# A two-layer hybrid decoder trunk in fp32 on one core: products of one width in runs, one PSUM bank less in each wino_job, and other numbers in the plan

## The chip, the cores and the metric

The kernel runs on one NeuronCore of a Trainium2 chip. The metric is the time of one execution on the device in microseconds; of several executions the median is taken. The engines are named as in the profile: PE (TensorE, matrix products; PEld are its weight loads), DVE (VectorE), ACT (ScalarE), POOL (GpSimd) and SP (SyncE, here only a queue that issues transfers).

## The reference, cut to what matters

Two layers, each of a mixer (retention and a Mamba-2 scan side by side, joined by gates) and a SwiGLU feed-forward, on 256 rows of 1024 columns, all in fp32.

```python
D_MODEL, SEQ, DEPTH = 1024, 256, 2

def hybrid_mixer(h, ...):
    u = h @ w_in
    q, k, v, g_ret, z, xbc, dt, gate_ret, gate_ssd = split(u)
    yr = retention(rotary(q), rotary(k) * RET_DK ** -0.5, v)
    o_ret = (silu(g_ret) * norm(yr)) @ ret_out
    xs, bm, cm = split(silu(causal_dwconv(xbc, conv_w, conv_b)))
    ys = ssd_scan(xs * dtp, dtp * a, bm, cm) + d_skip * xs
    o_ssd = (norm(ys * silu(z)) * ssd_norm_w) @ ssd_out
    return (sigmoid(gate_ret) * o_ret + sigmoid(gate_ssd) * o_ssd) @ w_o

def swiglu(h, w_gate_up, w_down):
    gate, up = split(h @ w_gate_up)
    return (silu(gate) * up) @ w_down

for l in range(DEPTH):
    h = h + hybrid_mixer(rmsnorm(h, norm_mix_w[l]), ...)
    h = h + swiglu(rmsnorm(h, norm_ffn_w[l]), w_gate_up[l], w_down[l])
return rmsnorm(h, final_norm_w)
```

## The kernel before

**Products.** Every fp32 operand is split into a high part (wh, xh) and a rest (wl, xl), and a product of two is the sum of three PE products: high by high, high by rest, rest by high. split_piece does this for each piece of a weight of 128x1024: ACT writes wh (L507), DVE writes wl as raw minus wh (L530). Pieces land in four buffers raw, and up to seven split pieces are held.

There are three ways in which a projection is made. In tm_jobs the activations are the stationary side and 512 or 352 columns of a weight move (mm3, L546 to L548). In **fm_job** the weight is stationary and the activations move; it is used for q, k, the convolution's channels and part of the feed-forward. High and rest of the activations lie beside each other in the tile xT, so one product of 512 columns (wh by high and rest, L1025, and L1028 for the last of a block) does two of the three, and one of 256 columns (wl by high, L1026) does the third into the first half of the same bank. A job has two blocks b of 16 products, each into one PSUM bank: for k = 0 to 6 a wide and a narrow one, and for k = 7 the narrow one first. The job's follower (gathered) lets ACT copy the second half of the bank and DVE add the first.

The third way is **seven**: a product of 2x2 blocks by seven products instead of eight (Strassen's scheme in Winograd's form), named "11", "t1", "t2", "22", "t3", "21" and "t4", of twelve PE products each in plain order. Each of them adds into a PSUM bank, a, b, c1 or c2; bank a is used by four in turn, and is copied to a tile u1, u2 or u3 of the pool sx (four buffers) before the next may add to it. wino_job combines these with additions on DVE (upper, first, third). wino_job is used once in each layer's mixer (the gate gs) and twice in each feed-forward. out_wino uses the same seven, but puts c1 and c2 into banks of its own (into).

**What sets the order.** The kernel is planned when it is built: each stream of work is a generator that yields operations with an engine, an assumed duration and a priority, and Flow runs them through a small model of the engines. At each free engine it takes the ready operation of the lowest priority number, and writes its instruction. The order of every engine's queue is so fixed in the program; on the chip each engine follows its own queue, and waits where an input isn't there yet. The model has one number for the time when the transfers will be free (transfer). Two kinds of transfers were not in it: the wb loads on POOL (load_wb, a fixed 4000 ns; eight of them) and the seg loads of ssd_chunk on SP (1500 on the queue and a fixed 5000 ns; sixteen of them). Each brings one row to all 128 partitions. Changes of these numbers move instructions, but add none.

PSUM has eight banks: six named acc, two named tr.

Of the kernel before, what the change touches and what calls it, by code (L numbers as in the profile page):

```python
# [16 lines left out]
P = 128  # L17
D = 1024
# [174 lines left out]
def trunk_kernel(  # L193
# [68 lines left out]
    sxS, new_sx = pooled(tp, (P, 512), F32, "sx", 4)  # L262
    segS, new_seg = pooled(tp, (P, HPG, P), F32, "seg", 2)
# [231 lines left out]
    def split_piece(raw, m, turn, pr, src=None):  # L495
# [26 lines left out]
        if src is not None:  # L522
            wl = yield Op("act", 0.833 * m + 92, negative, pr)
            yield Op("pool", 1050, lambda: add(wl), pr)
            yield fl.transfer(512 * m, 4 * m, 2.2) - ADDS
            return wh[:, :m], wl[:, :m]
# [9 lines left out]
    def splitter(turn, k, n, ev, job, src, sem):  # L536
        def land(raw, landed):
            yield landed
            wh, wl = yield from split_piece(raw, k * n, turn, job - 0.7, src)
            fl.release(sem)  # L540
            fl.set(ev, tuple(a.rearrange("p (k n) -> p k n", k=k) for a in (wh, wl)))
        return land
# [90 lines left out]
    def transposed(src, n, dst, i, t, pr, plain=None, slack=0.0):  # L633
# [11 lines left out]
        v = yield pe(110 * n, pr, emit)  # L645
# [31 lines left out]
    def seven_sums(ops, op, parts, tag, pr, plain=None):  # L677
# [6 lines left out]
        for n in range(2):  # L684
            for t in range(NT):
                yield (plain[n][t] if plain else op.ready[parts[n]][t])
        for n in range(2):
            for t in range(NT):
                if plain:
                    x[n, t] = yield plain[n][t]  # L690
                else:
                    xh, xl = (a[:, :, t * P : (t + 1) * P] for a in op.at(parts[n])[:2])
                    yield sxS
                    x[n, t] = new_sx("plain")
                    v = x[n, t].rearrange("p (j t) -> p j t", j=4)
                    yield tt(512, pr, v, xh.bitcast(F32), xl.bitcast(F32), ALU.add)
        x11, x12, x21, x22 = x[0, 0], x[1, 0], x[0, 1], x[1, 1]
# [203 lines left out]
    GOT = ("a", "b", "c1", "c2", "u1", "u2", "u3")  # L901

    def seven(j, pe_pr, ops, got, into={}):
# [6 lines left out]
        bank = {"11": "a", "t1": "b", "t2": "a", "22": "c1", "t3": "a", "21": "c2", "t4": "a"}  # L910
        after = {"11": "u1", "t2": "u2", "t3": "u3"}
        wait = {"t2": "u1", "t3": "u2", "t4": "u3"}
        box = {}

        def product(q):
# [7 lines left out]
            for k in range(4):  # L923
                wh, wl = yield evs[q][k // 2]

                def emit():
                    if first and k == 0:
                        box[name] = new_acc()
                    mm3(into[name]() if name in into else box[name], xh[:, k, :], xl[:, k, :], wh[:, k % 2, :], wl[:, k % 2, :],
                        first and k == 0, k == 3 and name not in into, skip_group_check=name == "a")  # L930
# [4 lines left out]
            if q in after:  # L935
                fl.spawn(copied(after[q]))
# [3 lines left out]
        def copied(name):  # L940
            yield sxS
            u = new_sx()
            yield act(512, j - 1, u, box["a"], AF.Copy, psum=True)
# [4 lines left out]
    def wino_job(ops, *posts):  # L948
# [4 lines left out]
        def upper():  # L953
# [53 lines left out]
    def fm_job(xT, post):  # L1007
# [4 lines left out]
        for b in range(2):  # L1012
            fsl = slice(b * P, (b + 1) * P)
            yield accS
            ps = None
            for k in range(8):
                for t in range(NT):
                    yield xT.ready[k // 4][t]
                wh, wl = yield evs[k // 4]

                def emit():
                    a = new_acc() if ps is None else ps
                    xh, _, x = xT.at(k // 4)
                    if k < 7:
                        nc.tensor.matmul(a, lhsT=wh[:, k % 4, fsl], rhs=x[:, k % 4, :, :], start=k == 0, stop=False)  # L1025
                    nc.tensor.matmul(a[:, :SEQ], lhsT=wl[:, k % 4, fsl], rhs=xh[:, k % 4, :], start=False, stop=False)  # L1026
                    if k == 7:
                        nc.tensor.matmul(a, lhsT=wh[:, k % 4, fsl], rhs=x[:, k % 4, :, :], start=False, stop=True)  # L1028
                    return a

                ps = yield pe(mm_cost(512) + mm_cost(256) + 5, pe_pr + 0.5, emit)
                if b == 1 and k % 4 == 3:
                    fl.release(hlS)
            if b == 0:
# [266 lines left out]
    def layer(l, mix, nxt, opening=None):  # L1301
# [75 lines left out]
        def steps():  # L1377
# [34 lines left out]
            ps = yield pe(240, pr, sums)  # L1412
# [13 lines left out]
            ps = yield pe(430, pr, sums_t)  # L1426
# [49 lines left out]
        def retention(hd, dst, q_ev, k_ev):  # L1476
# [15 lines left out]
            ps = yield pe(1290, pr, scores)  # L1492
# [149 lines left out]
        def xs_post(g, jj):  # L1642
            def post(ps, second, j):
# [18 lines left out]
                tps = yield pe(440, j, emit)  # L1662
# [15 lines left out]
        def ssd_scores(g):  # L1678
# [14 lines left out]
            ps = yield pe(650, pr, scores)  # L1693
# [23 lines left out]
        def ssd_chunk(g, t, lp, pr, dtt, acs, dec, dr, prm, cb, xs, x0_ev):  # L1717
# [8 lines left out]
            sg = yield Op("sp", 1500, bring, lp)  # L1726
            yield 5000.0
# [10 lines left out]
            yield tt(1024, lp, sg, sg, cb[:, 2 * t, :].unsqueeze(1).broadcast_to([P, HPG, P]), ALU.mult)  # L1738
            yield sxS
            xdt = new_sx("xdt")  # L1740
            yield tt(512, lp, h3(xdt), h3(xs[:, t, :]), hb(dtt, t * NH, g), ALU.mult)
            yield sxS
            tail = new_sx("tail")
            dsb = prm[:, 2, g * HPG : (g + 1) * HPG].unsqueeze(2).broadcast_to([P, HPG, HD])
            yield tt(512, lp, h3(tail), h3(xs[:, t, :]), dsb, ALU.mult)
            if t == 1:
# [8 lines left out]
                ips = yield pe(856, pr, inter)  # L1755
# [13 lines left out]
            yps = yield pe(1780, pr, intra)  # L1769
# [195 lines left out]
        def seven_job(kind, c, added):  # L1965
            if kind == "z":
                z_begins(c)
# [340 lines left out]
```

## Time and profile before

| | us |
|---|---|
| median of 3 runs | 1253.91 |
| lowest, highest | 1252.53, 1253.92 |
| the profiled execution's own time | 1254.38 |
| its span in the trace | 1252.6 |

The page of the profile begins with the span and each engine's busy time. A row of a group reads: line, engine, operation, output tile <- input tiles, shapes, xcount, then busy time in all, mean ns of one, and the engine's idle time just before them with what ended it. A PE product is pipelined: its shown duration (some 390 ns for 512 columns) is longer than its distance to the next one, so the distances between starts tell how densely products stand. A row of the timeline reads: start in us from the span's begin, duration, engine, line, operation, tiles, shapes, and how many it merges.

### The profile page before, as it was taken

Reading aid. Unit: us, or ns where it says so; the run is one execution under the profiler, and the core shown is the slowest. Engines: PE = TensorE matmul, PEld = TensorE weight load, DVE = VectorE, ACT = ScalarE, POOL = GpSimd, SP = SyncE. Lnnn points to the kernel's source line nnn. Section 1 sums busy time; section 2 is a strip of 40 time slices with the busy share of each in tenths; the row PEclk is TensorE's granted clock in tenths of the full one; section 3 lists DMA queues with packets and bytes.
Section 4 is the critical chain, followed back from the end, with each engine's and each line's share of the span. In section 5 each row is a group of like instructions: output and inputs, shape, how many; then the busy total and the mean of one; then the engine's idle time right before and its main releaser. Section 6 shows DMA issues by size and latency. Waiting matters only on the chain.

```text
span 1252.6 us, 17625 instructions
## 1 busy us (share of the span) xinstructions
PE 1241.2 (99%) x6293; PEld 1052.1 (84%) x6293; DVE 1108.7 (89%) x1519; ACT 880.7 (70%) x1304; POOL 72.0 (6%) x92
## 2 busy tenths in 40 slices
PE   9999999999999999999999999999999999999997
PEld 7889888888888778888888898888888888888886
DVE  6998889889999979999788888888899998899996
ACT  6966778786766566776586676878877674776753
POOL 0000000001012001001000000000010110010000
PEclk9999999999999999999999999999999999999999
DMA  8748565466777658877776475555676686677872
GB/s 314 252 133 287 163 207 154 164 236 134 254 235 218 230 176 237 293 209 219 258 254 230 117 253 170 185 172 163 216 182 238 240 233 216 211 216 252 294 201 86
DMA packets 76343, 266.27 MB, mean 213 GB/s; under 512 B 8768, under 2 KB 9536, under 8 KB 76256
## 3 DMA queue, kind: packets, MB, share of 16 engines
q1 hardware_dynamic: 68272, 237.12, 55.1%
q0 software_dynamic: 7552, 27.38, 11.8%
q8 instruction: 49, 0.80, 0.2%
q10 hardware_dynamic: 432, 0.66, 0.1%
q14 instruction: 38, 0.31, 0.1%
HBM read 262.96 MB, written 2.16 MB: 212 GB/s over the span
## 4 chain that ended last, share of the span: by engine, by line
PE 87%; DVE 4%; ACT 4%; issue 2%; DMA 2%; POOL 0%; POOLq 0%; DVEq 0%; ACTq 0%
PE acc L546 18%; PE acc L548 17%; PE acc L547 17%; PE acc L1025 15%; PE acc L1026 9%; PE tr L642 2%; PE acc L1028 2%; PE yps L1765 2%; DVE wl L530 2%; ACT wh L507 2%; PE acc L868 1%; DMA raw<-in_w_rw_dram 1%; ACT seg L1733 1%; DMA raws<-in_w_sw_dram 1%; PE acc L1487 1%
## 5 line engine op out<-in xcount | busy, mean ns | idle before, releaser
L530 DVE TENSOR_TENSOR wl<-raw,wh 128x1024 fp32r<-128x1024 f32 (+2 forms) x387 | 458.4, 1197 | 51.1 <-ACT wh L507 47.2
L507 ACT ACTIVATE wh<-raw 128x1024 fp32r<-128x1024 f32 (+2 forms) x387 | 396.8, 1037 | 137.9 <-PE acc L548 27.7
L1025 PE MATMUL acc<-xT,wh 128*128 128x512 f32 x840 | 304.9, 400 | 0.0
L1026 PE MATMUL acc<-xT,wl 128*128 128x256 f32 x960 | 251.2, 281 | 0.0
L546 PE MATMUL acc<-wh,xT 128*128 128x512 f32 (+1 forms) x568 | 220.4, 388 | 0.0
L547 PE MATMUL acc<-wl,xT 128*128 128x512 f32 (+1 forms) x568 | 216.2, 381 | 0.0
L548 PE MATMUL acc<-wh,xT 128*128 128x512 f32 (+1 forms) x568 | 216.2, 381 | 0.0
L1026 PEld LDWEIGHTS acc<-xT,wl 128*128 128x128 f32 x960 | 181.2, 189 | 10.4
L1025 PEld LDWEIGHTS acc<-xT,wh 128*128 128x128 f32 x840 | 158.0, 188 | 31.8
L547 PEld LDWEIGHTS acc<-wl,xT 128*128 128x128 f32 x568 | 106.8, 188 | 20.2 <-issue 1.0
L548 PEld LDWEIGHTS acc<-wh,xT 128*128 128x128 f32 x568 | 106.6, 188 | 19.6
L546 PEld LDWEIGHTS acc<-wh,xT 128*128 128x128 f32 x568 | 106.7, 188 | 19.3 <-issue 1.2
L507 ACT ACTIVATE wh<-raws 128x1024 fp32r<-128x1024 f32 x80 | 83.7, 1057 | 35.0 <-DVE raws L230 12.8
L530 DVE TENSOR_TENSOR wl<-raws,wh 128x1024 fp32r<-128x1024 f32 x80 | 96.4, 1220 | 9.2 <-ACT wh L507 9.0
L546 PE MATMUL acc<-wh,A 128*128 128x512 f32 x224 | 89.3, 399 | 0.3 <-DVE cc L230 0.2
L548 PE MATMUL acc<-wh,A 128*128 128x512 f32 x224 | 87.4, 390 | 0.0
L547 PE MATMUL acc<-wl,A 128*128 128x512 f32 x224 | 87.3, 390 | 0.0
L233 DVE SCALAR_TENSOR_TENSOR cc<-cc,cv 128x255 f32<-128x255 f32 (+1 forms) x144 | 67.2, 478 | 4.5 <-ACT cc L223 3.7
L223 ACT ACT_TABLE_LOAD x39 | 50.0, 1283 | 3.4 <-DVE cc L233 2.8
L546 PEld LDWEIGHTS acc<-wh,A 128*128 128x128 f32 x224 | 42.1, 188 | 9.9 <-ACT sil L223 1.0
L548 PEld LDWEIGHTS acc<-wh,A 128*128 128x128 f32 x224 | 42.0, 188 | 8.9
L547 PEld LDWEIGHTS acc<-wl,A 128*128 128x128 f32 x224 | 42.1, 188 | 8.5 <-issue 0.2
(201 smaller groups left out, 2057.2 us busy)
## 6 DMA issues: line engine op xcount, KB each, us to landing
raw<-in_w_tm_dram SPq DMA_DIRECT2D x100, 512.0 KB, 4.2
raw<-in_w_fm_dram SPq DMA_DIRECT2D x80, 512.0 KB, 4.3
raw<-in_w_gf_dram SPq DMA_DIRECT2D x40, 512.0 KB, 4.7
raw<-in_w_gate_up_dram SPq DMA_DIRECT2D x32, 512.0 KB, 6.3
raw<-in_w_down_dram SPq DMA_DIRECT2D x28, 512.0 KB, 4.6
raw<-in_w_gr_dram SPq DMA_DIRECT2D x24, 352.0 KB, 3.6
seg<-acs SPq DMA_DIRECT2D x16, 512.0 KB, 4.5
raw<-in_ret_out_dram SPq DMA_DIRECT2D x16, 512.0 KB, 3.8
```

The costliest lines, as they stand in the source:

```text
L223: return Op("act", cost, lambda: nc.scalar.activation(out=out, in_=in_, func=func, **kw), pr, TABLES.get(func))
L233: return Op("dve", 1.04 * n + 130, lambda: nc.vector.scalar_tensor_tensor(out=out, in0=in0, scalar=scalar, in1=in1, op0=op0, op1=op1), pr)
L507: nc.scalar.activation(out=wh[:, :m], in_=raw[:, :m], func=AF.Copy)
L530: nc.vector.tensor_tensor(out=wl[:, :m], in0=raw[:, :m], in1=wh[:, :m].bitcast(F32), op=ALU.subtract)
L546: nc.tensor.matmul(ps, lhsT=lh, rhs=rh, start=first, stop=False, **kw)
L547: nc.tensor.matmul(ps, lhsT=lh, rhs=rl, start=False, stop=False, **kw)
L548: nc.tensor.matmul(ps, lhsT=ll, rhs=rh, start=False, stop=last, **kw)
L642: nc.tensor.transpose(out=ps[:, j * P : (j + 1) * P], in_=src[:, j * P : (j + 1) * P], identity=ident)
L1025: nc.tensor.matmul(a, lhsT=wh[:, k % 4, fsl], rhs=x[:, k % 4, :, :], start=k == 0, stop=False)
L1026: nc.tensor.matmul(a[:, :SEQ], lhsT=wl[:, k % 4, fsl], rhs=xh[:, k % 4, :], start=False, stop=False)
L1028: nc.tensor.matmul(a, lhsT=wh[:, k % 4, fsl], rhs=x[:, k % 4, :, :], start=False, stop=True)
L1765: nc.tensor.matmul(ps[:, i * HD : (i + 1) * HD], lhsT=sg[:, i, :], rhs=xdt[:, i * HD : (i + 1) * HD], start=True, stop=True)
```

## The change

Four things are done together. Line numbers in the kernel after the change are 1 to 15 higher.

1. fm_job: the order in a block is now four wide products and four narrow ones of the first half of k, then four narrow and four wide ones of the second half. They are planned two at a time.
2. seven and wino_job: where it isn't into other banks, "22" adds into bank b, behind "t1". Before that, ACT copies "t1" to a further sx tile, ub, and "22" waits for it. The addition of c1 goes, and the job holds three banks, not four.
3. The plan's numbers: the wb loads on POOL and the seg loads now go through transfer (the seg load with 450 on the queue and 850 ahead), and groups of fp32 products cost a little more (transposes 113.5 instead of 110 each, and so on).
4. Two guards of the plan: sxG lets either seven_sums or the pair of chunks of one ssd_group take sx buffers; split_piece can release its source earlier (this is for pieces that the lists here don't name).

The core of the diff:

```diff
@@ load_wb
-        yield fl.transfer(4 * P * D) if eng == "sp" else 4000.0
+        yield fl.transfer(4 * P * D)
@@ seven
-        bank = {"11": "a", "t1": "b", "t2": "a", "22": "c1", "t3": "a", "21": "c2", "t4": "a"}
+        bank = {"11": "a", "t1": "b", "t2": "a", "22": "c1" if into else "b", "t3": "a", "21": "c2", "t4": "a"}
         after = {"11": "u1", "t2": "u2", "t3": "u3"}
         wait = {"t2": "u1", "t3": "u2", "t4": "u3"}
+        if not into:
+            after["t1"] = wait["22"] = "ub"
...
-            yield act(512, j - 1, u, box["a"], AF.Copy, psum=True)
+            yield act(512, j - 1, u, box[of], AF.Copy, psum=True)
@@ wino_job, upper
             yield tt(512, j, u2, b, u2, ALU.subtract)
-            c1 = yield got["c1"]
-            yield tt(512, j, u2, c1, u2, ALU.add)
             fl.release(accS)
             fl.spawn(posts[1](0, u2, j, sxS))
+            ub = yield got["ub"]
             u3 = yield got["u3"]
-            yield tt(512, j, u3, b, u3, ALU.subtract)
-            fl.release(accS)
+            yield tt(512, j, u3, ub, u3, ALU.subtract)
+            fl.release(sxS)
@@ fm_job
-            for k in range(8):
...
-                    if k < 7:
-                        nc.tensor.matmul(a, lhsT=wh[:, k % 4, fsl], rhs=x[:, k % 4, :, :], start=k == 0, stop=False)
-                    nc.tensor.matmul(a[:, :SEQ], lhsT=wl[:, k % 4, fsl], rhs=xh[:, k % 4, :], start=False, stop=False)
-                    if k == 7:
-                        nc.tensor.matmul(a, lhsT=wh[:, k % 4, fsl], rhs=x[:, k % 4, :, :], start=False, stop=True)
...
-                ps = yield pe(mm_cost(512) + mm_cost(256) + 5, pe_pr + 0.5, emit)
+            for half, wide in ((0, True), (0, False), (1, False), (1, True)):
...
+                    for k in (k0, k0 + 1):
+                        if wide:
+                            nc.tensor.matmul(box[0], lhsT=wh[:, k, fsl], rhs=x[:, k, :, :],
+                                             start=(half, k) == (0, 0), stop=(half, k) == (1, 3))
+                        else:
+                            nc.tensor.matmul(box[0][:, :SEQ], lhsT=wl[:, k, fsl], rhs=xh[:, k, :], start=False, stop=False)
+
+                for k0 in (0, 2):
+                    yield pe(2 * mm_cost(512 if wide else SEQ) + (5 if wide else 0), pe_pr + 0.5, lambda: emit(k0))
@@ ssd_chunk
-            sg = yield Op("sp", 1500, bring, lp)
-            yield 5000.0
+            sg = yield Op("sp", 450, bring, lp)
+            yield 850.0
+            yield fl.transfer(4 * P * D)
...
+            if t == 0:
+                yield sxG
             yield sxS
             xdt = new_sx("xdt")
...
             yield sxS
+            if t == 1:
+                fl.release(sxG)
```

What this does to the order of the queues is shown at three places. In all, the numbers of instructions of PE, POOL and SP stay; ACT has six copies more and six table loads fewer (40 to 34 in the program), DVE six additions fewer.

The first place is PE's queue at the start of the feed-forward's first fm_jobs in layer 0 (xT holds the activations; tr are transposes of the job before). Before the change:

```order
L1026 MATMUL acc<-xT,wl 128x256
L642 MATMUL tr<-cst,sil 128x128 x4
L1025 MATMUL acc<-xT,wh 128x512
L1026 MATMUL acc<-xT,wl 128x256
L1025 MATMUL acc<-xT,wh 128x512
L1026 MATMUL acc<-xT,wl 128x256 x2
L1028 MATMUL acc<-xT,wh 128x512
L1025 MATMUL acc<-xT,wh 128x512
```

And after it, at the same place:

```order
L1036 MATMUL acc<-xT,wh 128x512 x4
L1039 MATMUL acc<-xT,wl 128x256 x8
L646 MATMUL tr<-cst,sil 128x128 x4
L1036 MATMUL acc<-xT,wh 128x512 x8
L646 MATMUL tr<-cst,sil 128x128 x4
```

The alternation of wide and narrow has gone; the last four wide ones of a block and the first four of the next make a run of eight, and the transposes fall between runs.

The second place is ACT's queue at the first seven of the same feed-forward, where sx<-acc of 128x512 is the copy of a bank and wh<-... are splits of weights. Before the change:

```order
L223 ACTIVATE sx<-acc 128x512
L507 ACTIVATE wh<-cc 128x1024
L223 ACTIVATE C<-sil 128x512
L507 ACTIVATE wh<-cc 128x1024
L507 ACTIVATE wh<-raw 128x1024 x2
L223 ACTIVATE sx<-acc 128x512
L507 ACTIVATE wh<-raws 128x1024 x2
L507 ACTIVATE wh<-raw 128x1024 x2
L223 ACTIVATE sx<-acc 128x512
```

After it:

```order
L223 ACTIVATE sx<-acc 128x512
L508 ACTIVATE wh<-cc 128x1024
L223 ACTIVATE C<-sil 128x512
L508 ACTIVATE wh<-cc 128x1024
L223 ACTIVATE sx<-acc 128x512
L508 ACTIVATE wh<-raw 128x1024 x2
L223 ACTIVATE sx<-acc 128x512
L508 ACTIVATE wh<-raws 128x1024 x2
L508 ACTIVATE wh<-raw 128x1024 x2
L223 ACTIVATE sx<-acc 128x512
```

The copy of "t1" (the second sx<-acc) has come in between; the splits keep their order.

The third place is DVE's queue in layer 0's second half of the mixer, ahead of the last group's product ips, which PE makes from xdt (sr holds decay factors, C the group's xs, yps its first chunk's product). Before:

```order
L230 TENSOR_TENSOR C<-yps,tail 128x512
L233 SCALAR_TENSOR_TENSOR sil<-sil,rz,wb 128x512 x2
L530 TENSOR_TENSOR wl<-raw,wh 128x1024 x3
L230 TENSOR_TENSOR Y<-tr,Y 128x4x128
L530 TENSOR_TENSOR wl<-raw,wh 128x1024
L230 TENSOR_TENSOR Y<-tr,Y 128x4x128
L230 TENSOR_TENSOR xdt<-xdt,sr 128x512
```

After:

```order
L233 SCALAR_TENSOR_TENSOR sil<-sil,rz,wb 128x512 x2
L533 TENSOR_TENSOR wl<-raw,wh 128x1024 x3
L230 TENSOR_TENSOR Y<-tr,Y 128x4x128
L533 TENSOR_TENSOR wl<-raw,wh 128x1024
L230 TENSOR_TENSOR C<-yps,tail 128x512
L230 TENSOR_TENSOR xdt<-xdt,sr 128x512
```

The chunk's own addition, C<-yps, has moved from the front of the weights' splits to the place just ahead of xdt<-xdt,sr, and one transpose's follower (Y<-tr,Y) has moved behind it.

More of the change, by code (lines that the diff above doesn't have):

```diff
@@ L262, in trunk_kernel @@
     sxS, new_sx = pooled(tp, (P, 512), F32, "sx", 4)
+    sxG = Sem(1)
     segS, new_seg = pooled(tp, (P, HPG, P), F32, "seg", 2)
@@ L523, in split_piece @@
             wl = yield Op("act", 0.833 * m + 92, negative, pr)
+            if sem:
+                fl.release(sem)
             yield Op("pool", 1050, lambda: add(wl), pr)
@@ L538, in land @@
             yield landed
-            wh, wl = yield from split_piece(raw, k * n, turn, job - 0.7, src)
-            fl.release(sem)
+            wh, wl = yield from split_piece(raw, k * n, turn, job - 0.7, src, sem)
+            if src is None:
+                fl.release(sem)
             fl.set(ev, tuple(a.rearrange("p (k n) -> p k n", k=k) for a in (wh, wl)))
@@ L686, in seven_sums @@
                 yield (plain[n][t] if plain else op.ready[parts[n]][t])
+        if not plain:
+            yield sxG
         for n in range(2):
@@ L696, in seven_sums @@
                     yield tt(512, pr, v, xh.bitcast(F32), xl.bitcast(F32), ALU.add)
+        if not plain:
+            fl.release(sxG)
         x11, x12, x21, x22 = x[0, 0], x[1, 0], x[0, 1], x[1, 1]
@@ L929, in emit @@
                     mm3(into[name]() if name in into else box[name], xh[:, k, :], xl[:, k, :], wh[:, k % 2, :], wl[:, k % 2, :],
-                        first and k == 0, k == 3 and name not in into, skip_group_check=name == "a")
+                        first and k == 0, k == 3 and name not in into, skip_group_check=name in ("a", "b"))
                 yield pe(3 * mm_cost(512), pe_pr + 0.5, emit)
@@ L935, in product, with copied @@
             if q in after:
-                fl.spawn(copied(after[q]))
+                fl.spawn(copied(after[q], name))
             elif name not in into:
                 fl.set(got[name], box[name])
-        def copied(name):
+        def copied(name, of):
             yield sxS
             u = new_sx()
-            yield act(512, j - 1, u, box["a"], AF.Copy, psum=True)
+            yield act(512, j - 1, u, box[of], AF.Copy, psum=True)
             fl.set(got[name], u)
@@ L1014, in fm_job, with emit @@
             yield accS
-            ps = None
-            for k in range(8):
+            box = []
+            for half, wide in ((0, True), (0, False), (1, False), (1, True)):
                 for t in range(NT):
[L1018 to L1023, printed above, removed]
-                    if k < 7:
-                        nc.tensor.matmul(a, lhsT=wh[:, k % 4, fsl], rhs=x[:, k % 4, :, :], start=k == 0, stop=False)
-                    nc.tensor.matmul(a[:, :SEQ], lhsT=wl[:, k % 4, fsl], rhs=xh[:, k % 4, :], start=False, stop=False)
-                    if k == 7:
-                        nc.tensor.matmul(a, lhsT=wh[:, k % 4, fsl], rhs=x[:, k % 4, :, :], start=False, stop=True)
-                    return a
-                ps = yield pe(mm_cost(512) + mm_cost(256) + 5, pe_pr + 0.5, emit)
-                if b == 1 and k % 4 == 3:
+                    yield xT.ready[half][t]
+                wh, wl = yield evs[half]
+                def emit(k0):
+                    if not box:
+                        box.append(new_acc())
+                    xh, _, x = xT.at(half)
+                    for k in (k0, k0 + 1):
[6 more added lines that the diff above has]
+                    yield pe(2 * mm_cost(512 if wide else SEQ) + (5 if wide else 0), pe_pr + 0.5, lambda: emit(k0))
+                if b == 1 and (half, wide) in ((0, False), (1, True)):
                     fl.release(hlS)
+            ps = box[0]
             if b == 0:
@@ L1738, in ssd_chunk @@
             yield tt(1024, lp, sg, sg, cb[:, 2 * t, :].unsqueeze(1).broadcast_to([P, HPG, P]), ALU.mult)
+            if t == 0:
+                yield sxG
             yield sxS
@@ L1742, in ssd_chunk @@
             yield sxS
+            if t == 1:
+                fl.release(sxG)
             tail = new_sx("tail")
@@ L1753, in inter @@
                     return ps
-                ips = yield pe(856, pr, inter)
+                ips = yield pe(882, pr, inter)
                 yield tt(512, lp, h3(x0), h3(ips), hb(dec, 0, g), ALU.mult)
```

20 lines of the change are left out of this document (9 added, 11 removed).

## The prediction

> **What bounds the kernel now.** I read the page first, for the share of each engine and the chain that ended last.
>
> ```profile
> span 1252.6 us, 17625 instructions
> PE 1241.2 (99%) x6293; PEld 1052.1 (84%) x6293; DVE 1108.7 (89%) x1519; ACT 880.7 (70%) x1304; POOL 72.0 (6%) x92
> PEclk9999999999999999999999999999999999999999
> PE 87%; DVE 4%; ACT 4%; issue 2%; DMA 2%; POOL 0%; POOLq 0%; DVEq 0%; ACTq 0%
> ```
>
> TensorE (PE) is busy for 99% of the span at the full granted clock, and 87% of the last chain is its own work. To see how much it can still lose or win by waiting, I cut the span into head, middle and tail, and then listed what PE waited for.
>
> ```profile
> 0.00:6.03 6.03, 4.71 (x15) 1.00 0.60 193
> 6.03:1246.01 1239.98, 1236.50 (x6281) 1.00 0.68 213
> 1246.01:1252.60 6.59, 0.00 (x0) 0.72 0.21 80
> PE idle L2181 <- DVE mhalf L2158: 1.3, 1, 1.3
> PE tr L642 <- DVE sil L233: 1.1, 2, 0.8
> PE tr L642 <- ACT wh L507: 0.9, 1, 0.9
> PE ips L1752 <- DVE xdt L230: 0.5, 1, 0.5
> PE tr L642 <- DVE D L230: 0.4, 1, 0.4
> PE acc L546 <- DVE cc L230: 0.2, 1, 0.2
> ```
>
> The first three rows give stretch, its length, PE's busy time with its count, clock, DMA share and GB/s. Between the first product at 6.03 and the end of the last at 1246.01 PE is idle for 1239.98 - 1236.50 = 3.5 us. The other rows (who waited for whom; total, times, longest) name 3.1 us of it; the 1.3 us belong to the warm-up in the head. So the span is 6.0 head, 1236.5 products, 3.5 waits and 6.6 tail. DVE and ACT, with 11% and 30% of slack, cost nothing unless they make PE wait. **A change pays only by making the stream of products itself shorter, or by those 3.5 us.**
>
> Busy time says nothing of how densely products stand, so I went to the starts in the timeline. One job of fm_job has two blocks of 16 products, eight of 512 columns (wide, L1025 and L1028) and eight of 256 (narrow, L1026). L1028 stands once in each block.
>
> ```profile
> L1026 PE MATMUL acc<-xT,wl 128*128 128x256 f32 x960 | 251.2, 281 | 0.0
> L1028 PE MATMUL acc<-xT,wh 128*128 128x512 f32 x120 | 47.7, 397 | 0.0
> 480.09 0.40 PE L1028 MATMUL acc<-xT,wh 128*128 128x512 f32 x1
> ...
> 496.76 0.40 PE L1026 MATMUL acc<-xT,wl 128*128 128x256 f32 x2
> 497.00 0.40 PE L1028 MATMUL acc<-xT,wh 128*128 128x512 f32 x1
> 497.24 0.40 PE L546 MATMUL acc<-wh,xT 128*128 128x512 f32 x1
> 497.47 0.39 PE L547 MATMUL acc<-wl,xT 128*128 128x512 f32 x1
> 497.70 0.39 PE L548 MATMUL acc<-wh,xT 128*128 128x512 f32 x1
> 497.93 0.39 PE L546 MATMUL acc<-wh,xT 128*128 128x512 f32 x1
> ```
>
> There are 120 blocks (960 narrow products, 120 times L1028). From the L1028 at 480.09 to that at 497.00 lie exactly six blocks with nothing between them: 16.91 / 6 = **2.818 us a block**, or 0.352 us for a wide and a narrow one. The comparison comes from the end of the kernel, where the same widths stand in runs of one width.
>
> ```profile
> 1238.86 0.39 PE L546 MATMUL acc<-wh,C 128*128 128x512 f32 x1
> ...
> 1242.03 0.39 PE L548 MATMUL acc<-wh,Y 128*128 128x512 f32 x1
> 1242.26 0.28 PE L546 MATMUL acc<-wh,C 128*128 128x256 f32 x1
> 1242.37 0.28 PE L547 MATMUL acc<-wl,C 128*128 128x256 f32 x1
> ...
> 1245.73 0.28 PE L548 MATMUL acc<-wh,Y 128*128 128x256 f32 x1
> ```
>
> Fifteen wide products take 1242.26 - 1238.86 = 3.40 us, 0.2267 each; 29 narrow ones take 1245.73 - 1242.26 = 3.47 us, 0.1197 each. Sum 0.346, against 0.352 in alternation.
>
> **The products in runs.** The number of products is the same; their order in a block goes from fifteen changes of width to two. Eight wide and eight narrow ones at the pace of runs are 8 x 0.2267 + 8 x 0.1197 = 2.771 us. What is left are the two seams. Behind a narrow one, the wide starts at 497.00, 497.24, 497.47, 497.70 and 497.93 are 0.93 apart over four, where a run would have 0.907: this seam costs 0.02, and the third step is back at the pace of a run. At the other seam the first narrow step, 1242.26 to 1242.37, is 0.11, so 0.01 is won. New block: 2.771 + 0.02 - 0.01 = 2.781 us. That is 0.037 less than 2.818, times 120: **4.4 us off PE's own stream**, which nothing else can hide, since PE is the bound and its inputs are already waiting there (L1026's idle time is 0.0).
>
> Bounds of this term. Without any seam it is 0.047 x 120 = 5.6 us. If all four wide products behind a narrow run stay slow by the 0.01 of 497.00 to 497.24, 0.03 more a block are lost and 0.007 x 120 = 0.8 us remains. On the far side, if every wide one of these jobs took the 0.24 of that step wherever it stands, the block would be 8 x 0.24 + 0.958 = 2.878 us and the change would lose 7.2 us. Against that stands the first wide product of such a job behind a run of wide ones:
>
> ```profile
> 516.29 0.39 PE L1025 MATMUL acc<-xT,wh 128*128 128x512 f32 x1
> 516.51 0.28 PE L1026 MATMUL acc<-xT,wl 128*128 128x256 f32 x1
> 516.63 0.40 PE L1025 MATMUL acc<-xT,wh 128*128 128x512 f32 x1
> 516.86 0.28 PE L1026 MATMUL acc<-xT,wl 128*128 128x256 f32 x1
> ```
>
> It takes 0.22; the next one, behind a narrow one, 0.23. The slowness hangs on the neighbour, not on the job, so I take 4.4.
>
> The Trainium skill speaks against any gain here: TensorE: Matmul & The Clock Gate, section Back-to-back issue gap, gives the isolated gap of a warm product as columns / 2.4 + 2.5 ns, by the width alone, which makes 215.8 and 109.2 ns. By it the order would not matter and this term would be 0. The trace has 0.227 and 0.120 in runs, more than the page, and a step that depends on its neighbour.
>
> **The sevens.** Six jobs of wino_job (two on gs, four in the feed-forward) now copy "t1" out of PSUM with ACT, and "22" adds into that same bank; one DVE addition each goes.
>
> ```profile
> L223 ACT ACTIVATE sx<-acc 128x512 f32<-128x512 f32 x36 | 21.3, 593 | 11.2 <-PE acc L548 8.0 <-DVE C L230 2.2 <-DVE tail L230 0.8
> L230 DVE TENSOR_TENSOR sx<-acc,sx 128x512 f32<-128x512 f32 x36 | 24.5, 686 | 2.7 <-ACT sx L223 2.2 <-PE acc L548 0.4
> L223 ACT ACT_TABLE_LOAD x39 | 50.0, 1283 | 3.4 <-DVE cc L233 2.8
> ```
>
> ACT gains 6 x 0.593 = 3.6 us and, in the new order, loses six table loads of 1.283 (7.7 us); DVE loses 6 x 0.686 = 4.1 us. Neither is on PE's path: 0. The new wait is that of "22" for the copy. Between "t1" and "22" stands "t2", twelve wide products, 12 x 0.2267 = 2.7 us, while the copy takes 0.6 and may have one split of a weight (1.05) ahead of it. The same kind of wait exists already ("t2", "t3" and "t4" wait for a copy with one product between, 36 times), and no ACT sx stands among PE's waits above. So 0; without that cover it would be 0.6 plus what stands ahead in ACT's queue, some 1.6 us for each of six, 10 us at the far end. The freed bank brings nothing, for no wait above is for a bank but the 0.2 us of acc L546.
>
> **The account of transfers and fp32 groups.** These are only numbers in the plan; the instructions and bytes remain. They move transfers and small pieces of work.
>
> ```profile
> seg<-acs SPq DMA_DIRECT2D x16, 512.0 KB, 4.5
> wb<-in_ssd_norm_w_dram POOLq DMA_DIRECT2D x4, 512.0 KB, 6.9
> wb<-in_norm_ffn_w_dram POOLq DMA_DIRECT2D x2, 512.0 KB, 4.1
> ```
>
> The plan took 4.0 us for wb; it lands after 4.1 to 6.9. On SP a few seg loads change place with one or two weights, on POOL almost nothing. What can come of it is bounded by PE's waits. Of the 3.1 us the 0.9 (tr for ACT wh, in the opening) and the 1.1 (tr for DVE sil, at the two feed-forward norms) are a latency with the same rows around it in the new order: they stay. The other 1.1 us (ips, tr for D, acc L546) stand where rows move. They may go, or as many new ones may come: I count 0 and +-1.5 us. The guards sxG hold back work in the plan, not on the chip: 0.
>
> **The sum.** 1254.38 (this execution: 1252.6 span and 1.8 around it) - 4.4 = 1250.0. This execution stands 0.4 above the median of the runs shown, 1253.91; so the median after is 1249.6. A measurement of this kernel tells 0.2%, 2.5 us, from no change.
>
> **Rivals.** (1) *A product's step goes by its width and job alone*, and reordering gives nothing: 1253.9, same. For it speaks that 0.006 us a pair is less than the timeline's two digits and comes from means over 96 and 44 products; against it the rows at 516. Chance 0.13; the rule quoted above from the Trainium skill would be this case. (2) *The gain is given back in new waits*: the plan was balanced on a few tenths (the waits above are all under 1 us), and rows move at sixteen seg loads. Four waits like the 0.5 of ips give 1251.6, same. For it: in the new DVE order the scaled xdt still stands only a few rows ahead of its ips. Chance 0.09. (3) *Slower: the four sx buffers.* A seven now holds u1, ub, u2 and u3 at once, which is all four; before, it held three. If another stream still holds one, ACT's copy of u3 waits at the head of ACT's queue until u1 is used, which is after product "21"; the splits of weights queue behind it, and "t4" starts late by the addition 0.69, the activation 0.6, the copy 0.59 and three handovers of about 0.2: 2.4 us. It decides from three of the six sevens on: 1249.6 + 3 x 2.4 = 1256.8; all six, 1264.0. Against it:
>
> ```profile
> 499.95 0.69 DVE L230 TENSOR_TENSOR sil<-sx,sil 128x512 f32<-128x512 f32 x1
> 511.05 0.60 ACT L223 ACTIVATE sx<-acc 128x512 f32<-128x512 f32 x1 [0.29 <-PE acc L548]
> ```
>
> At the first seven of the feed-forward the last outside reader of an sx is done at 500.64, and u3 is copied at 511.05, ten microseconds later. Chance 0.05, and 0.03 more for the wide products at 0.24 (1261 us).
>
> **How the numbers follow.** The forecast keeps 0.70: 1249.6, own range 1246.8 (5.6 won, 1.5 of waits gone) to 1252.6 (2.6 won, halfway between 0.8 and 4.4, and 1.3 of new waits). The range has to reach to rival 1, most of it: 1247.0 to 1253.5. Faster by over 0.2% (below 1251.4): 0.70, which is the forecast less its upper edge, 0.04, and some cases of rival 2, 0.04. Same: 0.21. Slower (above 1256.4): 0.09, rival 3 with its companion and a stray 0.01.
>
> **What would show it.** Right: a block of these jobs in the new timeline at 2.78 us (first wide start to the next block's), narrow runs at 0.12, wide ones back at 0.227 from the third on; PE's busy time down by 4 to 5 us, its idle time between 3 and 5 us, DVE down 4 us with no effect. Wrong: a block at 2.82 (rival 1), new rows of 0.5 us and more among PE's waits (rival 2), or rows "PE acc <- ACT sx" of 2 us at the sevens (rival 3). A stall in the opening or at a norm that grows past 2 us would also break the sum.

## The result, and the profile after the change

| | before | after |
|---|---|---|
| median, us | 1253.8 (1252.53 to 1254.87, 8 runs) | 1257.28 (1255.76 to 1258.54, 8 runs) |
| ratio after to before, 95% interval | | 1.0028 [1.0017, 1.0039] |
| the profiled execution, its span | 1254.38, 1252.6 | 1257.84, 1255.6 |

The change makes the kernel 3.5 us slower, a little over what can be told from no change. The forecast was 1249.6 with a range up to 1253.5. Of all executions below, one of e3 (1366.42 us, at a granted clock of 0.85) and one of e4 (2525.56 us) fell far out of line with the others; the medians include them, the ratios and intervals do not.

The page after the change: span, each engine's busy time, and the shares of the chain that ended last.

```profile
span 1255.6 us, 17609 instructions
PE 1239.3 (99%) x6293; PEld 1051.0 (84%) x6293; DVE 1104.5 (88%) x1513; ACT 873.0 (70%) x1304; POOL 75.3 (6%) x92
PE 70%; DVE 14%; issue 6%; DMA 5%; ACT 4%; POOL 1%; POOLq 0%; ACTq 0%; DVEq 0%; SPq 0%
```

PE is busy for 1.9 us less than before and still for 99%, but the chain reads differently: PE's own work is 70% of it, not 87%, and DVE 14%, not 4%. That hints at waits, but a share of the chain doesn't count them. The same cut as before, middle and tail (the head is 6.03 again; stretch, length, PE's busy time with its count, clock, DMA share, GB/s):

```profile
6.03:1249.38 1243.35, 1234.56 (x6279) 1.00 0.67 213
1249.38:1255.60 6.22, 0.01 (x1) 0.67 0.22 84
```

In the middle PE is idle for 1243.35 - 1234.56 = 8.8 us, where it was 3.5. Set against before: products 1236.5 to 1234.6, **1.9 us won**; idle 3.5 to 8.8, **5.3 us lost**; tail 6.6 to 6.2, 0.4 won. That is +3.0, the difference of the spans. The rest of +3.5 lies around the span (2.2 us, where it was 1.8). What PE waited for, in the list after the change:

```profile
PE acc L552 <- DVE A L230: 3.2, 2, 1.8
PE idle L2196 <- DVE mhalf L2173: 1.3, 1, 1.3
PE ips L1769 <- DVE xdt L230: 1.3, 2, 1.0
PE tr L646 <- ACT wh L508: 1.3, 1, 1.3
PE tr L646 <- DVE sil L233: 0.9, 3, 0.3
PE tr L646 <- DVE D L230: 0.7, 2, 0.4
PE yps L1782 <- DVE Y L230: 0.5, 1, 0.5
PE acc L551 <- DVE wl L533: 0.4, 1, 0.4
PE acc L1499 <- DVE C L230: 0.3, 1, 0.3
PE acc L550 <- ACT sx L223: 0.2, 1, 0.2
```

Without the warm-up (1.3, L2196, in the head) these are 8.8 us against 3.1, and the first row, which did not exist before, is 3.2 of the 5.7 that came in. It stands once in each layer, at w_o, whose stationary side A is the transposed mixer output: in layer 0 at the first products (1.75 us), in layer 1 seven microseconds further into them (1.41 us, behind two splits in DVE's queue). Here is PE's queue in layer 0, in the timeline after the change (tr are the transposes of D, A the tile that their result goes to):

```profile
423.02 0.60 PE L646 MATMUL tr<-cst,D 128*128 128x128 f32 x4
...
425.28 0.63 PE L646 MATMUL tr<-cst,D 128*128 128x128 f32 x4 [0.28 <-DVE D L230]
425.66 0.47 PE L550 MATMUL acc<-wh,A 128*128 128x512 f32 x1
425.98 0.40 PE L551 MATMUL acc<-wl,A 128*128 128x512 f32 x1
428.13 0.50 PE L552 MATMUL acc<-wh,A 128*128 128x512 f32 x1 [1.75 <-DVE A L230]
```

And DVE's, from the same timeline, with the row in which ACT copies the transposes to A:

```profile
423.32 1.21 DVE L533 TENSOR_TENSOR wl<-raw,wh 128x1024 fp32r<-128x1024 f32 x1
424.19 0.58 ACT L223 ACTIVATE A<-tr 128x512 fp32r<-128x512 f32 x1
424.45 0.68 DVE L230 TENSOR_TENSOR D<-D 128x512 f32<-128x512 f32 x1
425.06 0.68 DVE L230 TENSOR_TENSOR D<-acc,D 128x512 f32<-128x512 f32 x1
425.66 1.21 DVE L533 TENSOR_TENSOR wl<-raw,wh 128x1024 fp32r<-128x1024 f32 x1
426.79 0.68 DVE L230 TENSOR_TENSOR D<-D 128x512 f32<-128x512 f32 x1
427.39 0.68 DVE L230 TENSOR_TENSOR A<-tr,A 128x512 fp32r<-128x512 f32 x1
```

The transposes of 423.02 are done at 423.6. DVE's follower A<-tr,A subtracts ACT's copy from them, so it could run when that copy ends, at 424.8. In DVE's queue it stands behind two splits and three operations on D, and it starts at 427.39. PE has one L550 and one L551 to do before it needs A's low part, and waits for 1.75 us. The same place in the timeline before the change, both engines:

```profile
422.31 0.63 PE L642 MATMUL tr<-cst,D 128*128 128x128 f32 x4 [0.43 <-DVE D L230]
...
425.54 0.69 DVE L230 TENSOR_TENSOR A<-tr,A 128x512 fp32r<-128x512 f32 x1
...
426.71 0.40 PE L548 MATMUL acc<-wh,A 128*128 128x512 f32 x1
```

Before, PE came to its L548 4.4 us after the start of the transposes (twelve other products stood between them and the first product with A, not six), and DVE to its follower 3.2 us after it, not 4.4. ACT's copy ended at 423.6 there (422.97 and 0.60), so DVE's queue set the follower's start in both. The follower was done at 426.2, half a microsecond ahead of its reader. DVE has 12% of slack over the span and none here.

The runs of one width, in the timeline after the change:

```profile
480.08 2.00 PE L1036 MATMUL acc<-xT,wh 128*128 128x512 f32 x8
481.92 1.11 PE L1039 MATMUL acc<-xT,wl 128*128 128x256 f32 x8
...
494.04 2.00 PE L1036 MATMUL acc<-xT,wh 128*128 128x512 f32 x8
```

Five blocks take 494.04 - 480.08 = 13.96 us, 2.792 each: 0.026 under the 2.818 of alternation, where 0.037 was forecast.

So the part that was to win, wins, though by less than forecast, and PE's new waits take more than that back. The experiments ask which part of the change brings the waits, and whether any part costs something by itself.

### The profile page after: what moved, and what is told of

The parts are those of the page before. It is cut to its first block, busy times and chain, and to the rows that moved or that the text cites. A ratio compares the mean times of both kernels' runs of the same rounds, so it can differ in the third digit from the quotient of the medians.

```text
span 1255.6 us, 17609 instructions
## 1 busy us (share of the span) xinstructions
PE 1239.3 (99%) x6293; PEld 1051.0 (84%) x6293; DVE 1104.5 (88%) x1513; ACT 873.0 (70%) x1304; POOL 75.3 (6%) x92
## 4 chain that ended last, share of the span: by engine, by line
PE 70%; DVE 14%; issue 6%; DMA 5%; ACT 4%; POOL 1%; POOLq 0%; ACTq 0%; DVEq 0%; SPq 0%
PE acc L1036 15%; PE acc L550 14%; PE acc L552 14%; PE acc L551 14%; PE acc L1039 8%; DVE wl L533 6%; ACT wh L508 2%; PE yps L1782 2%; PE tr L646 2%; DVE D L230 1%; DMA raw<-in_w_fm_dram 1%; ACT seg L1746 1%; DMA raw<-in_w_rw_dram 1%; DVE cc L233 1%; DMA raws<-in_w_sw_dram 1%
## 5 line engine op out<-in xcount | busy, mean ns | idle before, releaser
L1036 PE MATMUL acc<-xT,wh 128*128 128x512 f32 x960 | 249.4, 394 | 0.0
L550 PE MATMUL acc<-wh,xT 128*128 128x512 f32 (+1 forms) x568 | 221.1, 389 | 0.0
L551 PE MATMUL acc<-wl,xT 128*128 128x512 f32 (+1 forms) x568 | 216.0, 380 | 0.4 <-DVE wl L533 0.4
L1036 PEld LDWEIGHTS acc<-xT,wh 128*128 128x128 f32 x960 | 171.0, 189 | 28.8
L1039 PEld LDWEIGHTS acc<-xT,wl 128*128 128x128 f32 x960 | 131.0, 190 | 9.4 <-issue 0.5
L1039 PE MATMUL acc<-xT,wl 128*128 128x256 f32 x960 | 137.0, 284 | 0.0
L551 PEld LDWEIGHTS acc<-wl,xT 128*128 128x128 f32 x568 | 106.8, 188 | 20.7 <-issue 1.2
L550 PEld LDWEIGHTS acc<-wh,xT 128*128 128x128 f32 x568 | 106.7, 188 | 20.0 <-issue 1.2
L550 PE MATMUL acc<-wh,A 128*128 128x512 f32 x224 | 88.6, 396 | 0.0
L551 PE MATMUL acc<-wl,A 128*128 128x512 f32 x224 | 87.2, 389 | 0.0
L233 DVE SCALAR_TENSOR_TENSOR cc<-cc,cv 128x255 f32<-128x255 f32 (+2 forms) x144 | 67.5, 478 | 7.5 <-ACT cc L223 6.8
L550 PEld LDWEIGHTS acc<-wh,A 128*128 128x128 f32 x224 | 42.1, 188 | 8.5 <-ACT sil L223 0.4
L223 ACT ACTIVATE sil<-acc 128x512 f32<-128x512 f32 (+1 forms) x60 | 31.0, 526 | 26.0 <-PE acc L552 14.1
L551 PEld LDWEIGHTS acc<-wl,A 128*128 128x128 f32 x224 | 42.1, 188 | 8.3
```

The costliest lines, as they stand in the source:

```text
L223: return Op("act", cost, lambda: nc.scalar.activation(out=out, in_=in_, func=func, **kw), pr, TABLES.get(func))
L233: return Op("dve", 1.04 * n + 130, lambda: nc.vector.scalar_tensor_tensor(out=out, in0=in0, scalar=scalar, in1=in1, op0=op0, op1=op1), pr)
L550: nc.tensor.matmul(ps, lhsT=lh, rhs=rh, start=first, stop=False, **kw)
L551: nc.tensor.matmul(ps, lhsT=lh, rhs=rl, start=False, stop=False, **kw)
L1036: nc.tensor.matmul(box[0], lhsT=wh[:, k, fsl], rhs=x[:, k, :, :], start=(half, k) == (0, 0), stop=(half, k) == (1, 3))
L1039: nc.tensor.matmul(box[0][:, :SEQ], lhsT=wl[:, k, fsl], rhs=xh[:, k, :], start=False, stop=False)
```

## The experiments

All medians are compared with the kernel before on the same chip (1253.7 to 1253.8 us). "Idle" and "busy" are PE's in the middle cut, made in one trace of each as above; e2, with the products of before, is 0.9 us less busy than before, so differences of that size in one trace say nothing.

| run | median | ratio, 95% interval | idle | busy |
|---|---|---|---|---|
| before | 1253.8 | | 3.5 | 1236.5 |
| after | 1257.28 | 1.0028 [1.0017, 1.0039] | 8.8 | 1234.6 |
| e1 runs in the old plan | 1251.21 | 0.9978 [0.9969, 0.9987] | 3.4 | 1234.0 |
| e2 sevens alone | 1254.01 | 1.0002 [0.9993, 1.001] | 3.4 | 1235.6 |
| e3 account alone | 1263.95 | 1.0074 [1.0061, 1.0087] | 9.1 | 1240.4 |
| e4 runs in a new plan | 1264.2 | 1.0079 [1.0066, 1.0092] | 10.8 | 1239.5 |
| e5 after, one number | 1254.88 | 1.0008 [0.9999, 1.0017] | 5.5 | 1234.3 |
| e6 after, other numbers | 1252.23 | 0.9993 [0.9984, 1.0002] | 2.6 | 1233.9 |
| e7 fp32 groups alone | 1268.81 | 1.012 [1.0106, 1.0134] | 13.0 | 1241.7 |
| e8 transfers alone | 1257.6 | 1.0031 [1.002, 1.0041] | 5.0 | 1238.2 |
| e9 runs of two | 1251.62 | 0.9981 [0.9972, 0.999] | 2.6 | 1234.2 |
| e10 runs and sevens | 1251.1 | 0.9977 [0.9968, 0.9986] | 3.3 | 1233.5 |
| e11 all, planned otherwise | 1254.63 | 1.0008 [0.9999, 1.0017] | 5.3 | 1234.8 |

### e1: the runs, with the plan of before

The plan still yields eight steps of "one wide and one narrow product", so every queue stays as it was. Only what a step writes follows a table (1 is wide, the second number is k):

```diff
+    RUNS = [[(1, 0), (1, 1)], [(1, 2)], [(1, 3), (0, 0)], [(0, 1), (0, 2), (0, 3)],
+            [(0, 4), (0, 5), (0, 6)], [(0, 7), (1, 4)], [(1, 5)], [(1, 6), (1, 7)]]
-                    if k < 7:
-                        nc.tensor.matmul(a, lhsT=wh[:, k % 4, fsl], ...)
-                    nc.tensor.matmul(a[:, :SEQ], lhsT=wl[:, k % 4, fsl], ...)
+                    for wide, i in RUNS[k]:
+                        if wide: ...
```

> The kernel before with its plan untouched: every queue keeps its order, only inside a block of fm_job the products stand as four wide, eight narrow, four wide. Theory A (the denser stream is worth 120 x 0.027 = 3.2 us wherever it is used, and the loss came with the new plan): 1250.6 us, PE's waits 3 to 4 us without the warm-up. Rival B (a denser stream only brings PE sooner to the same inputs, so the gain comes back as waits): 1253 to 1254 us, waits 6 to 7 us.

1251.21 us, 2.6 less than before. The middle of its trace:

```profile
6.03:1243.37 1237.34, 1233.98 (x6279) 1.00 0.68 214
```

And the starts of two runs of wide products in its timeline, four blocks apart:

```profile
480.97 2.00 PE L1029 MATMUL acc<-xT,wh 128*128 128x512 f32 x8
...
492.14 2.00 PE L1029 MATMUL acc<-xT,wh 128*128 128x512 f32 x8
```

Four blocks in 11.17 us, 2.793 each, and PE's busy time is 2.5 us lower with the same idle time. The runs of one width alone are worth 2.6 us, by the products themselves. Rival 1, that a product's step goes by its own width and job alone, is out.

### e2: the sevens, with the plan of before

Only bank and copy in seven and wino_job, and the guard sxG, with which this was planned:

```diff
+        bank = {..., "22": "c1" if into else "b", ...}
+        if not into:
+            after["t1"] = wait["22"] = "ub"
```

> The kernel before with the sevens on three banks and the guard sxG, nothing else. Theory A: no new wait of PE at the sevens, within 1 us of before, 1253 to 1255 us, waits near 3 us. Rival C (the four sx buffers or the copy of t1 make PE wait): 1256 us and more, with rows of PE waiting for ACT sx.

1254.01 us, no difference; idle time as before, and no wait for a copy sx among PE's. The six copies, the six additions that go and the new wait cost and bring nothing that can be measured.

### e3, e7, e8: the account, whole and in its two halves

```diff
e8, transfers:
-        yield fl.transfer(4 * P * D) if eng == "sp" else 4000.0
+        yield fl.transfer(4 * P * D)
-            sg = yield Op("sp", 1500, bring, lp)
-            yield 5000.0
+            sg = yield Op("sp", 450, bring, lp)
+            yield 850.0
+            yield fl.transfer(4 * P * D)
e7, fp32 groups (eight numbers of this kind):
-        v = yield pe(110 * n, pr, emit)
+        v = yield pe(113.5 * n, pr, emit)
```

e3 has both; alternation and the old sevens stay.

> The kernel before with the new numbers for wb, seg and the fp32 groups, nothing else. Theory A (the plan made with these numbers has the new waits): no stream gain and some 5 to 7 us of new waits, 1257 to 1261 us, with PE waiting for DVE A in wo. If the numbers are harmless: 1253 to 1255 us.

> The kernel before with the new costs of the fp32 groups alone (a few ns to 60 ns a group). If so small a change of the plan's numbers already re-orders wo: 3 us and more of new waits, 1256 to 1259 us. If the loss of e3 came from the transfers' account: 1253 to 1254.5 us.

> The kernel before with wb and seg counted as transfers, alone. If the transfers' account brings the loss: 1259 us and more, with waits at the sevens of ret as in e3. If each re-planning rolls its own waits: 1255 to 1259 us, at other places than e7.

1263.95, 1268.81 and 1257.6 us. For e8 the time lies in the range of the second case, but its one large wait, 3.58 us in layer 1, is not at another place than e7's: it is for a copy sx in the sevens of the retention's output projection, where e3 and e7 wait too. For e3 and e7 I expected up to 1261 and 1259, and they are 3 and 10 us above. The wait for A at w_o, expected in e3, is not in its list; e7 has it. Both halves together (+10) cost less than one of them (+15). So there is no price per number; each set of numbers writes another order, with its own waits. In e7 the list of PE's waits begins so:

```profile
PE acc L546 <- ACT sx L223: 6.4, 2, 3.4
PE acc L548 <- DVE A L230: 2.8, 2, 1.4
```

The second row is the wait at w_o, as after the change. The first is new: in the seven of the retention's output projection, "t3" reuses bank a and waits until ACT has copied "t2" out of it. ACT's queue in that place of e7:

```profile
316.57 2.45 ACT L1733 ACTIVATE seg<-seg,ax 128x128 f32<-128x128 f32 x8 [4.47 <-DMA seg<-acs]
318.93 1.99 ACT L507 ACTIVATE wh<-raw 128x1024 fp32r<-128x1024 f32 x2
320.94 1.28 ACT L223 ACT_TABLE_LOAD   x1
322.24 1.06 ACT L223 ACTIVATE seg<-seg 128x1024 f32<-128x1024 f32 x1
323.20 0.58 ACT L223 ACTIVATE sx<-acc 128x512 f32<-128x512 f32 x1
```

A copy of 0.58 us on which PE hangs starts at 323.20. Its bank was full at 317.7, behind the last product of "t2" (317.32 below); in ACT's queue eight steps on a seg tile, for whose transfer ACT had waited 4.47 us, two splits, a table load and one more step on seg stand before the copy. The twelve products of "22" (317.56 to 320.5), which add into another bank, cover a part of that, and then PE waits. Before the change, too, a copy of this seven stands behind a table load and a seg step (it starts at 324.63), but its bank was full only at 322.5 and twelve products lay over it: PE's next product comes at 325.27, some 0.2 us late. And the wait in e7 costs more than its length. PE's timeline there:

```profile
317.32 0.40 PE L548 MATMUL acc<-wh,O 128*128 128x512 f32 x1
...
320.08 0.39 PE L548 MATMUL acc<-wh,O 128*128 128x512 f32 x1
323.83 0.80 PE L546 MATMUL acc<-wh,O 128*128 128x512 f32 x1 [3.36 <-ACT sx L223]
324.42 0.63 PE L547 MATMUL acc<-wl,O 128*128 128x512 f32 x1
...
328.69 0.63 PE L548 MATMUL acc<-wh,O 128*128 128x512 f32 x1
```

And the same stretch cut into pieces of 2 us, with the granted clock behind PE's busy time and its count:

```profile
322.00:324.00 2.00, 0.17 (x1) 0.75 0.90 270
324.00:326.00 2.00, 2.00 (x5) 0.50 0.67 254
...
328.00:330.00 2.00, 2.00 (x7) 0.55 0.43 53
330.00:332.00 2.00, 2.00 (x11) 1.00 0.70 236
```

Behind the wait of 3.36 us the granted clock is 0.50, and ten steps of 512 columns take 328.69 - 324.42 = 4.27 us, 0.427 each instead of 0.227: 2 us more in these ten alone. All slow steps here (2.9 us too long together) and behind the second such wait, 3.05 us in layer 1 (1.7 us), make most of the 5.2 us by which e7's busy time is above before's with the same products. Idle +9.5 and busy +5.2 make 14.7, and its span is 14.4 longer; in e3 +5.6 and +3.9 make the 9.5 of its span, in e8 +1.5 and +1.7 the 3.2.

### e4: the runs, planned two at a time, without the rest

The new fm_job as in the change, with the old sevens and the old account. The guard sxG stands with it, so what it does to the order is not told apart here; together with the sevens (e2) it cost nothing.

> The kernel before with the runs of one width planned two at a time and the guard, old account and old sevens. If planning the runs anew is what brings the waits: 1256 to 1258 us with waits of 8 to 9 us, as after. If the account brings them: 1250 to 1251.5 us with waits of 3 to 4 us.

1264.2 us, 6 us above even the worse of the two cases. The products are e1's (the same runs), the time is 13 us above e1's: idle +7.4, busy +5.5, with the clock at 0.50 again behind a wait of 2.80 us at ips and one of 1.72 us at a copy sx that follows it (it stands at 0.50 from 330 to 338 us). So planning the runs two at a time, with the guard, costs, by the order that comes of it, five times what the runs bring.

### e5 and e6: the change with other thresholds of the plan

e5 changes one number of the changed kernel, the slack that the plan gives to the transposes of the mixer's output mT:

```diff
-    SLOW, MT_SLACK = 1500.0, 800.0
+    SLOW, MT_SLACK = 1500.0, 600.0
```

> The kernel after with one number of its plan changed: the transposes of mT, ahead of wo, are planned as ready 0.6 us behind their input, not 0.8. No operation is added or removed. Theory A (the loss sits in the order that the plan wrote at a few places, the largest being wo's first products, 3.2 us of waits for DVE A in two layers): these waits fall below 1 us in sum, 1254 to 1255.2 us. Rival D (DVE is too loaded at that place under the new kernel, whatever the order): the waits stay at 2 us and more, 1256.5 to 1258 us.

e6 has 800 there, and five others of this kind changed:

```diff
-    LATE = 2500.0
-    SLOW, MT_SLACK = 1500.0, 800.0
-    ZS_PR, SAVE, DEC_AT = 1.0, 2000.0, 9000.0
-    APARTS, SUMS_PR = {}, 3.5
-    RET_FIRST, RET_PR = (decS, new_dec), 0.0
+    LATE = 2000.0
+    SLOW, MT_SLACK = 1000.0, 800.0
+    ZS_PR, SAVE, DEC_AT = 0, 2000.0, 9000.0
+    APARTS, SUMS_PR = {}, 2.5
+    RET_FIRST, RET_PR = (decS, new_dec), 1.0
```

> The kernel after with five numbers of its plan changed (delays of transposes 1.0 instead of 1.5 us, scores 2.0 instead of 2.5 us, three priorities), all operations the same. Theory A: waits of PE down from 8.8 to 3 to 5 us, 1251.5 to 1254 us, so the runs' gain of some 3 us shows under the new numbers too. Rival D: 1256 us and more.

Both times are as expected. In e5 the wait at w_o is gone, and part of it comes back one step earlier, at the transposes themselves:

```profile
PE tr L646 <- DVE D L230: 1.9, 2, 1.1
```

3.2 us of acc for A go, tr for D rises from 0.7 to 1.9, idle falls from 8.8 to 5.5 and the time by 2.4 us. In e6 idle falls to 2.6, below what was expected and below before's, and the time is 1.5 us under before's, with an interval that still includes no change. Its trace is of its fastest execution (1250.95). All instructions of the change are in both: what it lost was lost by the order alone.

### e9: runs of two

As e1, with another table: wide 0 1, narrow 0 1, wide 2 3, narrow 2 to 5, wide 4 5, narrow 6 7, wide 6 7.

```diff
+    RUNS = [[(1, 0), (1, 1)], [(0, 0), (0, 1)], [(1, 2), (1, 3)], [(0, 2), (0, 3)],
+            [(0, 4), (0, 5)], [(1, 4), (1, 5)], [(0, 6), (0, 7)], [(1, 6), (1, 7)]]
```

> The plan of before, untouched, with the products of a block in runs of two and four columns widths: wide 0 1, narrow 0 1, wide 2 3, narrow 2 to 5, wide 4 5, narrow 6 7, wide 6 7. Nothing but PE's order inside a block differs from the run with 4, 8 and 4. Theory A: the loss hangs on each seam behind a narrow product, by the steps that stand in the trace of the changed kernel (first wide steps behind a narrow run 233, 236, 228, 233 ns, narrow ones 113, 119, 120): a block then takes 930 + 2 x 469 for the wide and 2 x 232 + 472 for the narrow ones, 2.804 us against 2.818 in alternation and 2.792 in runs of eight, so 1.7 us less than before: 1252.1. Theory B: what is won needs a long run, so runs of two are as slow as alternation: a block of 2.818, 1253.8.

1251.62 us. The four wide ones that span two blocks mark the period:

```profile
480.91 1.09 PE L1029 MATMUL acc<-xT,wh 128*128 128x512 f32 x4
...
492.11 1.09 PE L1029 MATMUL acc<-xT,wh 128*128 128x512 f32 x4
```

Four blocks in 11.20 us, 2.800 each, between alternation and runs of eight as theory A had it (2.804). The medians of e1 and e9 are 0.4 us apart, within their intervals. Most of what is won comes with runs of two and four already.

### e10 and e11: versions that might beat both

e10 joins e1 and e2. e11 has the sevens, the account and the guard sxG of the change, but writes the runs from steps of one wide and one narrow product, as e1 does (planned with 2 ns beside the products where before had 5), leaves out the earlier release in split_piece, and sets two thresholds (MT_SLACK 0, SLOW 1700).

> The plan of before with the runs inside a block of fm_job and with the sevens of the change (t1 copied to ub, 22 adds into bank b) and their guard; no other number is changed. Theory A: the two parts do not touch each other, since each alone kept PE's waits at 3.0 us: 1251.2 to 1251.5, PE's waits about 3. Theory B (any further change of the plan costs some us of new waits): above 1253.

> All instructions and all numbers of the change (sevens, transfers, fp32 groups), but the products of a block planned in pairs as before and written in runs, and two of the plan's thresholds (MT_SLACK 0, SLOW 1700) chosen so that the two feed-forward and mixer places that wait in the changed kernel have work before them. Theory A (what the change lost is only the order that the plan wrote): the waits come back to 2 to 3.5 us and the time to that of the runs alone or a little below, 1250.0 to 1251.7. Theory B (the new numbers or the sevens cost something of their own): above 1253.5.

e10: 1251.1 us, as theory A; with e1 the fastest here, and not to be told from it. e11: 1254.63, my theory A falls: idle is 5.3, with 2.4 us of tr for D at w_o and 1.1 of ips. Its time lies in theory B's range, but that the new numbers or the sevens cost something of their own does not follow: its busy time is that of after, the sevens are free in e2 and e10, and the excess is waits again, at places where e6, with the same instructions, has few. Choosing thresholds by reasoning about two places did not give a good order.

## Why the prediction was wrong, point by point

- **PE bounds the kernel, and a change pays only by its products or its waits.** Right, and it is how the loss reads: products 1.9 us shorter, idle 5.3 longer. "DVE and ACT, with 11% and 30% of slack, cost nothing unless they make PE wait" is right in its condition; the share says nothing about whether it is met. At w_o DVE works without a gap while PE waits for it. (Two sums of the prediction are 0.1 off: 1253.91 - 4.4 is 1249.5, and the delay in rival 3 adds up to 2.5. Nothing hangs on either.)
- **Runs of one width: mechanism right, term too large.** Forecast 4.4 us; e1 measured 2.6, with the interval 1.6 to 3.9. By the block, 2.781 was forecast and 2.792 came, 3.1 us in 120 blocks. The seams were the part mis-sized: a wide run was to take 1.834 us and takes 1.841, a narrow one 0.948 and takes 0.952 (medians in the trace after the change). The bounds given for the term, 0.8 to 5.6, held. "The third step is back at the pace of a run" does not hold: the medians of the wide steps behind a narrow run are 233, 236, 228, 233 and 231 ns, and only then 227 (over some 70 such places in the trace after the change). One seam of four products, read to two digits, could not show a fifth step.
- **The sevens: 0.** Right (e2, e10), the cover by "t2" included. Rival 3, the sx buffers, falls: no wait of 2 us at these sevens in e2 or after. The waits for a copy sx in e3, e4, e7 and e8 are at the retention's projection, which the sevens' change leaves alone, and come from what stands ahead of the copy in ACT's queue (in e4 and e7 also a transfer that ACT waits for there, 2.24 and 4.47 us).
- **The account: "I count 0 and +-1.5 us". This is the step that failed.** It took the waits that exist, 3.1 us in all and 1.1 of them where rows move, as the bound on both sides: "They may go, or as many new ones may come". Existing waits bound what a new order can win. What it can lose depends on the cover, the other work that the reader's engine has to do between each writer and its reader, which the list of waits does not show, because a covered wait is not in it. The idle time rose by 5.3 us, in e3, e4 and e7 by 5.6 to 9.5. At w_o in layer 0 the cover could have been counted in the order: twelve products between the first transposes and the first product with A before, six after, 2.7 against 1.4 us of PE's time, with DVE's follower one split and one addition later. The prediction looked at places that waited already.
- **The cost of an edit was put down to what it does in its own lines.** The guards and the steps of two products were set to 0 or not counted, as changes "in the plan, not on the chip". e4 shows the opposite: with the same products as e1 it is 13 us slower, all of it order and the clock behind the waits.
- **Rival 1** falls (e1, e9). **Rival 2**, the gain given back in new waits, is what happened, in kind; it was priced at four waits of 0.5 us and had a chance of 0.09. The single waits of 1.4 and 1.8 us at w_o are larger than the 0.5 allowed for, and with them the gain is lost, not halved. The forecast's sign was wrong for that reason; a slower kernel had 0.09 in all, and for other causes.

Not settled: why the plan, with an account nearer to the traced durations, writes orders with more waits. e3, e7 and e8 differ from before only in these numbers, and all three are slower. Which part of the change brings the waits at w_o is open too: of the parts alone, only e7 has them, and e3, which holds e7's numbers, has not. Whether new thresholds would make the account pay was tried in e5, e6 and e11 only, together with the rest.

## What to carry to other kernels

Where a plan or a scheduler writes the queues, a changed duration or a finer step is a change of the whole order: price it by the cover of each reader behind its writer in the new order (here the products between a transpose and the first use of its result), not by the waits of the old profile. To find what an idea is worth by itself, write it into the old order first (here a table inside a step that the plan doesn't see): that gave 2.6 us, where the same products planned anew lost 10. And a bounding engine at 99% with 3 us of idle time has little to win from a better order, and a good deal to lose.

## What the runs showed of the hardware

- A product's step depends on its neighbours' width. Behind a narrow run a wide step is 4 to 9 ns too long in four of the next five steps (233, 236, 228, 233, 231 against 227), and the first narrow one behind a wide run is short (113 against 120). A pair takes 0.352 us in alternation (2.818 a block), 0.350 in runs of two and four (2.800) and 0.349 in runs of eight (2.792).
- A wait of PE halves its clock afterwards, from a length on. In e7 a gap of 3.75 us between starts did (above). In e3 a shorter one was enough, though the first steps behind it were still quick:

```profile
325.31 0.39 PE L548 MATMUL acc<-wh,Y 128*128 128x512 f32 x1
327.70 0.50 PE L546 MATMUL acc<-wh,Y 128*128 128x512 f32 x1 [2.00 <-ACT sx L223]
...
328.52 0.63 PE L546 MATMUL acc<-wh,Y 128*128 128x512 f32 x1
...
331.91 0.40 PE L548 MATMUL acc<-wh,Y 128*128 128x512 f32 x1
```

  The gap of 2.39 us is followed, 0.8 us after it ended, by 3.4 us of steps of 0.43 (granted clock 0.50). The gap of 2.15 us at w_o after the change (425.98 to 428.13) left the clock at 1.00, and so did one of 2.21 us in e4 (952.21 to 954.42). So the waits that cost more than themselves begin between these lengths here, in e3 with eight steps of 0.43 instead of 0.227, 1.6 us; so few cases don't make a threshold. The Trainium skill, TensorE: Matmul & The Clock Gate, section Part 1: The HAM clock gate, has the clock halved after an idle window of about 3.4 us, with windows that run freely. Half speed, and its length of about one window in e3, agree with that (in e7 it lasted some 6 us); the gap of 2.39 us, shorter than a window, does not agree with a whole idle window being needed.
